# Nine small tiles instead of ten ahead of the weight tiles: where matmul operands begin in SBUF

## The chip, the core and the metric

The kernel runs on one core of a Trainium2 chip. The metric is the device time of one execution in microseconds (us); a lower time is better. A core has a matrix engine (TensorE; PE in the profile, with its weight loads as PEld), a vector engine (VectorE, DVE), an activation engine (ScalarE, ACT), GpSimd (POOL) and a queue engine that issues most transfers (SyncE, SP). They work side by side on SBUF, an on-chip memory of 128 partitions; matmul results go to PSUM. A tile takes the same byte range in every partition, and the addresses below are those within a partition.

## The reference

One layer of a streaming encoder, for 256 positions of width 2048, all in float32:

```python
x = x + 0.5 * swiglu(rms_norm(x, ffn1_norm), ffn1_w_gate, ffn1_w_up, ffn1_w_down)
h = rms_norm(x, mix_norm)
u, q, k, v = split(h @ w_in)
y_ssm = s5_mixer(u, ...)                       # diagonal complex state space, then a GLU
y_sb = stick_breaking_attention(rms_norm(q), rms_norm(k), v)
x = x + concat(rms_norm(y_ssm), rms_norm(y_sb)) @ w_out
x = x + 0.5 * swiglu(rms_norm(x, ffn2_norm), ffn2_w_gate, ffn2_w_up, ffn2_w_down)
gate = sigmoid(rms_norm(x, ple_norm) @ w_ple_gate)
x = x + rms_norm((p @ w_ple_proj) * gate, ple_post_norm)
```

The two feed-forward blocks (2048 to 5632 and back) hold most of the arithmetic, then `w_in`, `w_out` and `w_ple_gate`.

## The kernel before

Every large product is done as three products of float32r halves. A float32 value is split into a high part (rounded to float32r, a form of float32 that TensorE streams in one pass) and a low part, the rest; high x high, low x high and high x low are added up in PSUM. `split` (line 178) does it: ScalarE copies the source into the high tile (L181), VectorE subtracts that from the source into the low tile (L184). Weights come from HBM in tiles `raw` of 128 x 4 x 512 floats, one MB each, issued by SyncE; each half of such a tile becomes `whi` and `wlo` of 128 x 2 x 512. Activations stand as `nhi`/`nlo` or `hhi`/`hlo`, 128 x 4 x 256, turned so that 128 x 128 blocks of them are the stationary operand (`lhsT`) and the weights the moving one (`rhs`). In the GLU alone the weights are stationary and 256 columns of activations move (L1369, L1373, L1378).

`gemm_half` (line 298) issues, for a half weight tile, 12 matmuls of 512 columns: L305 and L306 with `whi`, L310 with `wlo`. `Seven` (from line 446) is a scheme with seven products for a 2 x 2 block of tiles, where VectorE adds up weight tiles first (L487) and the matmuls stand at L480, L481 and L483. The feed-forward blocks use both forms by turns. In each (j, t) of these loops the three lines are issued once:

```python
for j in range(2):
    for t in ts:
        nc.tensor.matmul(ps[t], lhsT=lh, rhs=hi[:, j, cols], start=start and j == 0, stop=False)
        nc.tensor.matmul(ps[t], lhsT=ll, rhs=hi[:, j, cols], start=False, stop=False)
for j in range(2):
    for t in ts:
        nc.tensor.matmul(ps[t], lhsT=lh, rhs=lo[:, j, cols], start=False, stop=stop and j == 1)
```

Smaller work on TensorE: transposes with the identity as moving operand (L392, L1207), sums over partitions with ones as moving operand (L1299), attention masks (L1234: `ident_r` stationary, `late_r` moving), and ten filler matmuls near the end (L1556: `ident_r` stationary, `pT` moving) while the last mean is worked out. GpSimd scales one 128 x 1 tile there (L1549).

**Where tiles lie.** Pools are laid out in SBUF one behind the other, in the order in which lines 52 to 56 open them, and each tile takes a multiple of 32 bytes. Ahead of the weights stand, in bytes per partition: 1024 of scratch for transfers (`dynamic_dma_scratch_size=1024`), four built-in constants of 32, then the pool `const` with `ident`, `ones`, `late_r`, `ident_r`, `tri_r`, `all_r` of 512 each, `gains` (354 floats, 1416, takes 1440) and `rho4` (128), then the pool `small`: tiles of 8 floats, 32 bytes, given out in turn by `small()` (line 82) for sums of squares, roots and the like. With ten of them the sum is 1024 + 128 + 3072 + 1440 + 128 + 320 = 6112 = 95 x 64 + 32. Every tile behind it takes a multiple of 64 bytes, and all offsets into one that a matmul uses (512 bytes for a 128-column block, 2048 for a 512-column row) are multiples of 64 as well. So in the kernel before, every weight, activation and sum that TensorE reads begins 32 bytes past a multiple of 64. The six 512-byte tiles of `const` begin at 1152 = 18 x 64 and are at multiples of 64.

Of the kernel before, what the change touches and what calls it, by code (L numbers as in the profile page):

```python
# [33 lines left out]
def layer_kernel(ctx: ExitStack, tc: tile.TileContext, a: dict, shapes: dict, out: bass.AP):  # L34
# [15 lines left out]
    assert TT == 2 and NP == 64 and HC == 16 and DH == P and NC == 64 and SW == NH * DH  # L50

    cpool = ctx.enter_context(tc.tile_pool(name="const", bufs=1))
    smp = ctx.enter_context(tc.tile_pool(name="small", bufs=10))
    wp = ctx.enter_context(tc.tile_pool(name="wts", bufs=4))
    actp = ctx.enter_context(tc.tile_pool(name="act", bufs=1))
    comp = ctx.enter_context(tc.tile_pool(name="com", bufs=1))
# [1605 lines left out]
```

## Time and profile before

| | |
|---|---|
| median of 3 runs | 1849.6 us (1848.7 to 1849.92) |
| profiled execution, its own time | 1849.88 us |
| its span, first to last instruction | 1847.8 us |
| TensorE busy | 1835.1 us, 99% of the span |
| VectorE busy | 1460.7 us, 79% |
| ScalarE busy | 1027.3 us, 56% |
| mean granted TensorE clock | 0.999 |
| HBM read | 373.46 MB, 209 GB/s over the span |

A matmul's busy time in the profile runs from its start to its modelled end and overlaps the next one's; the distance between starts is the pace. The timeline lists instructions with their start and duration in us; equal ones that follow each other are merged into one row with their number behind an x. The table of busy time by stretch gives, for a stretch of the span: its length; busy time and number of instructions (x) of PE, PEld, DVE, ACT and POOL in this order, of those engines that have any; the granted clock; the DMA engines' busy share; GB/s.

### The profile page before, as it was taken

How to read it: one execution, taken by the hardware profiler on the slowest of the kernel's cores; microseconds unless marked ns; L12 is line 12 of the kernel's file. 1: busy time of each engine (PE TensorE's matmuls, PEld its weight loads, DVE VectorE, ACT ScalarE, POOL GpSimd, SP SyncE). 2: the span in 40 equal slices, each digit the busy share in tenths (PEclk: the TensorE clock that was granted, in tenths of full speed). 3: DMA queues.
4: the chain of work that ended last, by engine and by line, in shares of the span. 5: the costliest groups of instructions: out<-in, count | busy, mean ns of one | idle time of the engine just before them, and what ended most of it. 6: DMA issues, size and time to landing. Idle time of an engine off the chain costs nothing.

```text
span 1847.8 us, 23946 instructions
## 1 busy us (share of the span) xinstructions
PE 1835.1 (99%) x9032; PEld 1518.8 (82%) x9032; DVE 1460.7 (79%) x1718; ACT 1027.3 (56%) x1187; POOL 65.1 (4%) x108
## 2 busy tenths in 40 slices
PE   9999999999999999999999999999999999999998
PEld 7888888778888888888898888888888888888887
DVE  8967664998888977687566798989898978887665
ACT  7444443655555656365685465555555555565654
POOL 0011000000000000010021000000000000000000
PEclk9999999999999999999999999999999999999999
DMA  9888868566756567675636776665656675656663
GB/s 332 283 273 281 251 213 247 178 228 203 242 189 221 193 217 249 190 263 166 216 139 218 221 266 213 242 206 198 218 198 221 208 242 187 223 190 220 207 220 125
DMA packets 232307, 406.36 MB, mean 220 GB/s; under 512 B 26784, under 2 KB 50720, under 8 KB 231904
## 3 DMA queue, kind: packets, MB, share of 16 engines
q1 hardware_dynamic: 227824, 392.81, 64.2%
q0 software_dynamic: 3648, 10.62, 1.8%
q8 instruction: 70, 1.15, 0.2%
q10 hardware_dynamic: 720, 1.41, 0.2%
q14 instruction: 45, 0.37, 0.1%
HBM read 373.46 MB, written 11.93 MB: 209 GB/s over the span
## 4 chain that ended last, share of the span: by engine, by line
PE 92%; DVE 3%; ACT 1%; DMA 1%; SPq 1%; issue 1%; DVEq 0%; ACTq 0%
PE acc L305 18%; PE acc L310 18%; PE acc L306 18%; PE aux L305 7%; PE aux L306 7%; PE aux L310 7%; PE acc L480 2%; PE acc L481 2%; PE acc L483 2%; PE aux L483 2%; PE aux L480 2%; PE aux L481 2%; SPq L1170 1%; DVE wlo L184 1%; DMA raw<-in_w_in 1%
## 5 line engine op out<-in xcount | busy, mean ns | idle before, releaser
L181 ACT CAST whi<-raw 128x1024 fp32r<-128x1024 f32 x639 | 667.5, 1051 | 679.3 <-PE acc L306 377.2
L184 DVE TENSOR_TENSOR wlo<-raw,whi 128x1024 fp32r<-128x1024 f32 x639 | 772.8, 1224 | 295.9 <-ACT whi L181 287.9
L305 PE MATMUL acc<-whi,nhi 128*128 128x512 f32 x1232 | 483.0, 392 | 2.1 <-ACT whi L181 1.6
L306 PE MATMUL acc<-whi,nlo 128*128 128x512 f32 x1232 | 480.0, 390 | 0.0
L310 PE MATMUL acc<-wlo,nhi 128*128 128x512 f32 x1232 | 340.7, 389 | 0.2 <-DVE wlo L184 0.2
L305 PEld LDWEIGHTS acc<-whi,nhi 128*128 128x128 f32 x1232 | 231.5, 188 | 52.6 <-ACT whi L181 3.1
L310 PEld LDWEIGHTS acc<-wlo,nhi 128*128 128x128 f32 x1232 | 231.3, 188 | 48.6 <-DVE wlo L184 0.6
L306 PEld LDWEIGHTS acc<-whi,nlo 128*128 128x128 f32 x1232 | 231.6, 188 | 47.0
L306 PE MATMUL acc<-whi,hlo 128*128 128x512 f32 x376 | 146.5, 390 | 0.0
L305 PE MATMUL acc<-whi,hhi 128*128 128x512 f32 x376 | 146.4, 389 | 0.0
L181 ACT CAST shi<-sum 128x1024 fp32r<-128x1024 f32 x108 | 113.5, 1052 | 43.1 <-DVE sum L487 39.4
L306 PE MATMUL aux<-whi,hlo 128*128 128x512 f32 x344 | 133.9, 389 | 0.0
L305 PE MATMUL aux<-whi,hhi 128*128 128x512 f32 x344 | 133.9, 389 | 0.0
L184 DVE TENSOR_TENSOR slo<-sum,shi 128x1024 fp32r<-128x1024 f32 x108 | 131.4, 1222 | 0.5 <-ACT shi L181 0.5
L310 PE MATMUL acc<-wlo,hhi 128*128 128x512 f32 x376 | 114.8, 390 | 0.2 <-DVE wlo L184 0.2
L310 PE MATMUL aux<-wlo,hhi 128*128 128x512 f32 x344 | 105.9, 389 | 0.0
L306 PE MATMUL aux<-whi,nlo 128*128 128x512 f32 x240 | 93.4, 389 | 0.0
L305 PE MATMUL aux<-whi,nhi 128*128 128x512 f32 x240 | 93.4, 389 | 0.0
L310 PEld LDWEIGHTS acc<-wlo,hhi 128*128 128x128 f32 x376 | 70.5, 188 | 15.5 <-DVE wlo L184 1.0
L306 PEld LDWEIGHTS acc<-whi,hlo 128*128 128x128 f32 x376 | 70.6, 188 | 14.9 <-DVE hlo L184 0.3
L305 PEld LDWEIGHTS acc<-whi,hhi 128*128 128x128 f32 x376 | 70.6, 188 | 14.6
L305 PEld LDWEIGHTS aux<-whi,hhi 128*128 128x128 f32 x344 | 64.6, 188 | 13.4
(345 smaller groups left out, 2164.8 us busy)
## 6 DMA issues: line engine op xcount, KB each, us to landing
raw<-in_ffn_w_up SPq DMA_DIRECT2D x88, 1024.0 KB, 5.9
raw<-in_ffn_w_down SPq DMA_DIRECT2D x88, 1024.0 KB, 5.1
raw<-in_ffn_w_gate SPq DMA_DIRECT2D x86, 1024.0 KB, 6.3
raw<-in_w_in SPq DMA_DIRECT2D x32, 1024.0 KB, 5.7
raw<-in_w_out SPq DMA_DIRECT2D x16, 1024.0 KB, 5.1
raw<-in_w_ple_gate SPq DMA_DIRECT2D x16, 1024.0 KB, 5.2
hT<-mid SPq DMA_DIRECT2D x160, 64.0 KB, 3.5
h<-mid SPq DMA_DIRECT2D x176, 32.0 KB, 3.7
```

The source lines that it names most:

```text
L181: copy = nc.scalar.copy(hi, src)
L184: nc.vector.tensor_tensor(out=lo, in0=src, in1=hi.bitcast(F32), op=ALU.subtract)
L305: nc.tensor.matmul(ps[t], lhsT=lh, rhs=hi[:, j, cols], start=start and j == 0, stop=False)
L306: nc.tensor.matmul(ps[t], lhsT=ll, rhs=hi[:, j, cols], start=False, stop=False)
L310: nc.tensor.matmul(ps[t], lhsT=lh, rhs=lo[:, j, cols], start=False, stop=stop and j == 1)
L480: nc.tensor.matmul(ps, lhsT=lh[j], rhs=hi[:, j], start=begin and j == 0, stop=False)
L481: nc.tensor.matmul(ps, lhsT=ll[j], rhs=hi[:, j], start=False, stop=False)
L483: nc.tensor.matmul(ps, lhsT=lh[j], rhs=lo[:, j], start=False, stop=z in final and j == 1)
L1170: nc.sync.dma_start(zt[0][p1 : p1 + HC, z], sv[p0 : p0 + HC, r % 2 * 2 + r // 2])
```

## The change

One number: the pool `small` gets nine tiles in place of ten.

```diff
     cpool = ctx.enter_context(tc.tile_pool(name="const", bufs=1))
-    smp = ctx.enter_context(tc.tile_pool(name="small", bufs=10))
+    smp = ctx.enter_context(tc.tile_pool(name="small", bufs=9))
     wp = ctx.enter_context(tc.tile_pool(name="wts", bufs=4))
```

The sum ahead of the weights becomes 6080 = 95 x 64. Every tile behind the pool moves down by 32 bytes and begins at a multiple of 64; the tiles of `const` stay where they are. The small tiles are given out in turn among nine places. The instructions, their order on every engine and their waits are those of before, but for one wait: L1549 on GpSimd, whose output tile now lies where another tile was, waits for an earlier ScalarE instruction than before.

## The prediction

> **What bounds the kernel now.** I first read the page's shares of busy time and its chain of work that ended last: whichever engine holds that chain sets the time.
>
> ```profile
> PE 1835.1 (99%) x9032; PEld 1518.8 (82%) x9032; DVE 1460.7 (79%) x1718; ACT 1027.3 (56%) x1187; POOL 65.1 (4%) x108
> ...
> PE 92%; DVE 3%; ACT 1%; DMA 1%; SPq 1%; issue 1%; DVEq 0%; ACTq 0%
> ```
>
> TensorE is it. But a pipelined matmul counts as busy past the start of the next, so busy time says nothing of pace. For pace I take a stretch without a pause from the table of busy time by stretch; its first columns are the stretch, its length, and TensorE's busy time with the number of matmuls.
>
> ```profile
> 1095.00:1515.00 420.00, 420.00 (x1853) 347.33 (x1852) 377.94 (x368) 229.93 (x237) 4.34 (x8) 1.00 0.66 217
> ```
>
> TensorE never stands still there, its granted clock is 1.00, and a matmul begins every 420.00/1853 = 0.2267 us. The timeline of TensorE shows that this is no mean of fast and slow ones. Its first column is the start:
>
> ```profile
> 1449.23 0.39 PE L483 MATMUL acc<-wlo,hhi 128*128 128x512 f32 x1
> 1449.46 0.39 PE L480 MATMUL aux<-whi,nhi 128*128 128x512 f32 x1
> 1449.69 0.39 PE L481 MATMUL aux<-whi,nlo 128*128 128x512 f32 x1
> 1449.92 0.39 PE L480 MATMUL aux<-whi,nhi 128*128 128x512 f32 x1
> 1450.14 0.39 PE L481 MATMUL aux<-whi,nlo 128*128 128x512 f32 x1
> ...
> 948.83 0.28 PE L1369 MATMUL acc<-hhi,whi 128*128 128x256 f32 x1
> ...
> 950.15 0.28 PE L1373 MATMUL acc<-hlo,whi 128*128 128x256 f32 x1
> ```
>
> Matmuls of 512 columns start every 0.227 us. The 256-column ones of the GLU (12 of them from the first row shown to the last, so 11 intervals) take 1.32/11 = 0.120 us each. From the two widths: (226.7 - 120.0)/256 = 0.4167 ns per column, and 226.7 - 512 x 0.4167 = **13.3 ns that each matmul pays whatever its width**. At this pace that is exactly 32 columns, or 128 bytes of a float32 row: two pieces of 64 bytes. All these matmuls read a moving and a stationary operand that begin 32 bytes past a multiple of 64. How much of the 13.3 ns goes with that offset is the whole question.
>
> **The change part by part.** It removes no instruction, adds none and moves none on any engine. It moves the addresses of everything allocated behind the small tiles by 32 bytes, and alters one wait.
>
> *The wait.* L1549, GpSimd's scale of a 128x1 tile in the tail, waits for an earlier ScalarE instruction than before. It waits in fact for VectorE:
>
> ```profile
> POOL sm L1549 <- DVE sq L1542: 355.0, 1, 355.0
> ```
>
> So this is worth nothing: L1542 still ends when it ends. Nine tiles in place of ten bring no other new wait.
>
> *The addresses under TensorE.* How many matmuls are concerned? The same table restricted to one line, over the whole span, first for L305, then for L480:
>
> ```profile
> 0.00:1848.00 1848.00, 863.16 (x2210) 415.13 (x2210) 1.00 0.66 220
> ...
> 0.00:1848.00 1848.00, 147.43 (x378) 70.98 (x378) 1.00 0.66 220
> ```
>
> L306 and L310 are issued as often as L305, L481 and L483 as often as L480: 3 x 2210 + 3 x 378 = 7764, of which 12 have 256 columns (the last block's second half, which `gemm_resident` does in two parts): 7752 of 512. The GLU issues L1369, L1373 and L1378 64 times each, so 192 of 256 columns.
>
> No row of before has a settled stream of 512-column float32r matmuls on operands that begin at a multiple of 64, so the saving is bounded. The **upper end** comes from the nearest streams with hardly any fixed cost, fp32 matmuls whose moving operand (the identity, the ones) begins at a multiple of 64:
>
> ```profile
> 731.31 0.93 PE L392 MATMUL aux<-ident,x 128*128 128x128 f32 x7
> ...
> 972.12 0.60 PE L1299 MATMUL aux<-ones,sqg 128*128 128x128 f32 x4
> ```
>
> The last one's own duration is in the group's row (minimum, median and maximum in ns): 0.27 us for L392, and as much for L1299.
>
> ```profile
> L392 PE MATMUL aux<-ident,x x8: 270/272/273, 731.3 to 732.1; 128*128 128x128 f32 x8
> ```
>
> So the starts lie (0.93 - 0.27)/6 = 0.110 and (0.60 - 0.27)/3 = 0.110 us apart. If such a record streams its 128 columns twice, that is 106.7 ns and 2.5 to 3 ns fixed. So at most 13.3 - 2.5 = 10.8 ns per matmul can go. These rows are another data type, though, and one of their operands does lie at the odd 32 bytes.
>
> The Trainium skill ("TensorE: Matmul & The Clock Gate", section "Back-to-back issue gap") gives N/2.4 + 2.5 ns for a warm matmul, with no term for where an operand begins; that is 215.8 ns for 512 columns where this trace has 226.7. By that figure as an estimate for the aligned kernel, the sum would be that of the upper end.
>
> The **other end** comes from the few float32r matmuls whose operands both begin at a multiple of 64 already, the masks (L1234, 256 columns read as the same 128 twice):
>
> ```profile
> 892.50 0.40 PE L1234 MATMUL aux<-late_r,ident_r 128*128 128x256 f32 x2
> 892.74 0.59 PE L1240 MATMUL aux<-q,k 128*128 128x256 f32 x2
> ```
>
> Two of them take 0.24 us, 0.120 each to within 0.005: no quicker than the misaligned GLU. They come in pairs behind other work and restart their row midway, so they don't show a settled stream, but they forbid counting on the upper end.
>
> I take a value between: **one of the two 64-byte pieces goes.** A row of 2048 bytes that begins 32 bytes off touches 33 pieces of 64 bytes, one that begins on the boundary 32; one piece is 16 columns, 6.67 ns. This reading is an inference from the fixed cost being a whole number of such pieces at both widths. It gives 7752 x 6.67 = 51.7 us and 192 x 6.67 = 1.3 us, together 53.0.
>
> *What is late next.* VectorE makes every low half of a weight tile, and is the next fullest engine:
>
> ```profile
> 340.00:510.00 170.00, 167.28 (x736) 137.88 (x736) 158.46 (x157) 94.57 (x98) 4.39 (x8) 1.00 0.68 220
> ```
>
> In 340 to 510 us VectorE is busy 158.5 of 170 (93%) and TensorE already waits 2.7; in 1095 to 1515 it is 377.9 of 420 (90%) with TensorE never idle. These 590 us hold 590/1848 of the gain, 16.9 us. With 2.9% less time VectorE would stand at 96% and 93% there. Nothing given back and all of it are the ends; I take a third, 5.6 us, since the longer stretch has no wait today.
>
> *The addresses under the others.* ScalarE, VectorE and the DMAs use the shifted tiles too. All that is not TensorE holds 8% of the chain, and DMA engines are busy 66% of the span in the rows above; a change of a few per cent either way stays under TensorE, except in the 590 us, where VectorE's spare 7 to 10% is the cover. I put nothing for them.
>
> Sum against the profiled execution (span 1847.8, its own time 1849.88; the median of the runs shown, 1849.6, is 0.3 less): 1849.9 - 53.0 + 5.6 = **1802.5**.
>
> **The rivals.**
>
> *The whole excess goes* (upper end). 10.8 x 7944 = 86 us; 590/1848 of it, 27 us, lies where VectorE is nearly full, and half of that might come back: 1849.9 - 86 + 14 = 1778, or 1764 with nothing given back. For it: the fp32 rows. Against it: the mask rows.
>
> *The change doesn't do what it says for time.* The 13.3 ns may belong to something that aligned operands pay as well, such as the load of new weights that runs beside every matmul. For it: the mask rows at 0.120. Then 1849.9 stays. The Trainium skill speaks for this one ("SBUF — State Buffer", section "Specifications (TRN2)"): it gives SBUF lines of 16 bytes, and an operand 32 bytes past a multiple of 64 begins on such a line already, so nothing would change; no row here shows the size of a line.
>
> *Slower: the stream no longer settles.* After a pause TensorE's starts are wider for some ten matmuls before they fall into 0.227:
>
> ```profile
> 153.10 0.40 PE L306 MATMUL acc<-whi,nlo 128*128 128x512 f32 x1
> ...
> 154.73 1.08 PE L310 MATMUL acc<-wlo,nhi 128*128 128x512 f32 x4
> ...
> 1838.84 2.05 PEld L1556 LDWEIGHTS aux<-pT,ident_r 128*128 128x128 f32 x9 [0.24 <-issue]
> ```
>
> From 153.10 to 154.73 there are seven intervals of 0.233. The tail's filler matmuls, whose stationary operand already begins at a multiple of 64 while the moving one doesn't, show (2.05 - 0.19)/8 = 0.2325 between weight loads, and don't settle within ten. So the pace depends on how the weight load and the moving operand meet in time, and the present 32-byte offset may be what lets them settle. If aligned streams stay at 0.233, that is 6.1 ns more: 1849.9 + 7752 x 6.1 ns = 1897. It decides as soon as the settled pace is above 0.2267. Against it: the filler's operands differ in offset from each other, the changed kernel's don't.
>
> **How the numbers follow.** One piece saved (the forecast, 1802, from 1790 to 1830 with the give-back and partial savings): 0.42. All of it (1764 to 1785): 0.25. No change, within 0.2% (3.7 us, about what a measurement of this kernel can tell from none): 0.18. Never settling, 1897: 0.15. That makes faster 0.67, same 0.18, slower 0.15. The range leaves out the last: from 1764, the upper end with nothing given back, to 1852, no change with its spread.
>
> **What would show it.** Right: in 1095 to 1515 us of the changed profile some 1909 matmuls per 420 us (0.220), GLU matmuls at 0.1133, VectorE's share up by about 3 points, small new waits of TensorE for L184 around 340 to 510. All gone: 0.216 and 0.109. No change: 0.2267 and 0.120. Slower: 0.231 or more, uneven. I am wrong in kind, not size, if the pace per matmul stays and the time moves: then another engine or the DMAs felt the addresses, and the rows of L181, L184 or the time to landing must show it.

## The result and the profile after

The changed kernel takes **1848.46 us** (median of 14 runs, 1847.95 to 1849.69), the kernel before, timed beside it, 1848.93 us (14 runs, 1848.06 to 1850.41). The ratio of the two is **0.9997, 95% interval 0.9989 to 1.0006**: no change, where 1802 was forecast. The profiled execution took 1848.89 us with a span of 1846.8.

The shares of busy time and the chain of the changed kernel stand as before: TensorE holds the chain.

```profile
PE 1833.7 (99%) x9032; PEld 1517.5 (82%) x9032; DVE 1459.7 (79%) x1718; ACT 1027.3 (56%) x1187; POOL 62.6 (3%) x108
...
PE 94%; DVE 2%; DMA 1%; SPq 1%; ACT 1%; issue 0%; DVEq 0%; ACTq 0%
```

The table by stretch answers the question directly:

```profile
340.00:510.00 170.00, 167.28 (x737) 137.79 (x737) 158.97 (x158) 94.80 (x98) 4.39 (x8) 1.00 0.67 220
1095.00:1515.00 420.00, 420.00 (x1852) 347.19 (x1851) 377.51 (x368) 230.37 (x237) 4.34 (x8) 1.00 0.66 217
```

In 1095 to 1515 us 1852 matmuls begin where 1853 began: 420.00/1852 = 0.2268 us each. In 340 to 510 there are 737 for 736. The timeline shows the single starts, of 512 columns and of the GLU's 256:

```profile
1449.11 0.39 PE L480 MATMUL aux<-whi,nhi 128*128 128x512 f32 x1
1449.33 0.39 PE L481 MATMUL aux<-whi,nlo 128*128 128x512 f32 x1
1449.56 0.39 PE L480 MATMUL aux<-whi,nhi 128*128 128x512 f32 x1
...
948.24 0.28 PE L1369 MATMUL acc<-hhi,whi 128*128 128x256 f32 x1
...
949.80 0.28 PE L1373 MATMUL acc<-hlo,whi 128*128 128x256 f32 x1
```

0.227 us again, and 1.56/13 = 0.120 for the GLU. The 13.3 ns beyond the columns are all still there; this is what the prediction gave for its rival of no change, "0.2267 and 0.120". Nothing was gained and lost again elsewhere.

For the comparisons below I sum up all distances between starts that follow a matmul of 512 columns, or of the 496 or 480 that stand for them in two runs (7773 in each trace: the 7752 large ones of the prediction, the fillers and a few more), in two parts: the mean of those up to 250 ns, which is the pace without a pause, and what the longer ones, in which TensorE waited or did other work, hold beyond that mean. Worked out from the start times in the traces, for all kernels of this study that hold the layer (the kernel before, timed again beside each of the others, took 1848.9 to 1850.0):

```
kernel         pace, ns   longer ones hold, us   time, us (median)
before           226.8          14.8             1848.93
after            226.8          14.5             1848.46
nine_odd         226.8          14.4             1849.31
unequal          232.8          12.0             1892.77
cut16            221.9          26.0             1823.72
cut32half        223.9          22.2             1834.27
quarter_half     224.0          17.6             1830.23
quarter_all      215.8          39.4             1790.4
```

### The profile page after: what moved, and what is told of

It reads as the page before. It is cut to its first block, busy times and chain, and to the rows that moved or that the text cites. A ratio compares the mean times of both kernels' runs of the same rounds, so it can differ in the third digit from the quotient of the medians.

```text
span 1846.8 us, 23946 instructions
## 1 busy us (share of the span) xinstructions
PE 1833.7 (99%) x9032; PEld 1517.5 (82%) x9032; DVE 1459.7 (79%) x1718; ACT 1027.3 (56%) x1187; POOL 62.6 (3%) x108
## 4 chain that ended last, share of the span: by engine, by line
PE 94%; DVE 2%; DMA 1%; SPq 1%; ACT 1%; issue 0%; DVEq 0%; ACTq 0%
PE acc L305 19%; PE acc L310 19%; PE acc L306 19%; PE aux L305 7%; PE aux L306 7%; PE aux L310 7%; PE acc L480 3%; PE acc L481 3%; PE acc L483 3%; PE aux L480 2%; PE aux L481 2%; PE aux L483 2%; SPq L1170 1%; DVE wlo L184 1%; DMA raw<-in_ffn_w_up 1%; PE aux L1124 0%
## 5 line engine op out<-in xcount | busy, mean ns | idle before, releaser
L184 DVE TENSOR_TENSOR wlo<-raw,whi 128x1024 fp32r<-128x1024 f32 x639 | 771.6, 1221 | 296.3 <-ACT whi L181 289.6
L305 PE MATMUL acc<-whi,nhi 128*128 128x512 f32 x1232 | 482.7, 392 | 2.6 <-ACT whi L181 1.6
L305 PEld LDWEIGHTS acc<-whi,nhi 128*128 128x128 f32 x1232 | 231.2, 188 | 53.3 <-ACT whi L181 3.2
L305 PE MATMUL acc<-whi,hhi 128*128 128x512 f32 x376 | 146.3, 389 | 0.0
L305 PE MATMUL aux<-whi,hhi 128*128 128x512 f32 x344 | 133.9, 389 | 0.0
L305 PE MATMUL aux<-whi,nhi 128*128 128x512 f32 x240 | 93.4, 389 | 0.0
L310 PEld LDWEIGHTS acc<-wlo,hhi 128*128 128x128 f32 x376 | 70.5, 188 | 15.2 <-DVE wlo L184 0.6
L306 PEld LDWEIGHTS acc<-whi,hlo 128*128 128x128 f32 x376 | 70.6, 188 | 14.8 <-DVE hlo L184 0.2
L305 PEld LDWEIGHTS acc<-whi,hhi 128*128 128x128 f32 x376 | 70.6, 188 | 14.7
L310 PEld LDWEIGHTS aux<-wlo,hhi 128*128 128x128 f32 x344 | 64.6, 188 | 13.5
```

Of the source, the lines that this page charges most:

```text
L184: nc.vector.tensor_tensor(out=lo, in0=src, in1=hi.bitcast(F32), op=ALU.subtract)
```

## Experiments

What the fixed 13.3 ns belong to had three answers left: a cost that every float32r matmul pays wherever its operands lie; a cost of lying off some boundary, hidden in the changed kernel by something else that the change did; or a cost that hangs on how the two operands lie **to each other**. The last was open because the change moves both by the same 32 bytes. By the order and sizes of the pools `whi`, `wlo`, `nhi`, `nlo`, `hhi`, `hlo`, `shi` and `slo` all begin at 224 modulo 256 before (`whi` at 47072, `nhi` at 79840) and at 192 after; the tiles of `const` begin at 128 in both.

Six of the runs are streams by themselves: a loop of matmuls on a moving operand `mv` and a stationary one `st`, each in one tile, with no layer around them, each run once. Blocks of one kind follow each other, so a block's pace is the distance from its row's start to the next row's, over its count. The code of these streams is shown shortened: letters stand for the offsets of each loop, and `...` for what stays as it was.

**m_offsets.** Both operands begin at 128 modulo 256; `a` and `b` shift them, in floats.

```diff
+for i in range(200):
+    mm(ps, lhsT=st[:, i%4*128 + a : i%4*128 + a + 128], rhs=mv[:, i%4*512 + b : i%4*512 + b + 512], start=True, stop=True)
```

> No layer is computed: eight streams of 200 float32r matmuls of 512 columns, alike but for where the moving and the stationary operand begin past a multiple of 64 bytes (moving/stationary: 0/0, 32/32, 32/0, 0/32, 4/0, 0/4, 16/16, 60/60 bytes). Theory A, the 13.3 ns belong to something every float32r matmul pays (its weight load, say): all eight settle at 0.2267 us. Theory B, only offsets within a 16-byte line matter: the three with 4 or 60 bytes are slower by one line, 4 columns, 1.7 ns, the other five stand at 0.2267. Theory C, the filler's 0.2325 was its unequal offsets: 32/0 and 0/32 stand at 0.2325, the equal ones at 0.2267.

The timeline of its TensorE; the blocks are, in bytes of moving/stationary shift, 0/0, 32/32, 32/0, 0/32, 4/0, 0/4, 16/16, 60/60:

```profile
9.74 48.17 PE L35 MATMUL b<-mv,st 128*128 128x512 f32 x200 [9.74 <-ACT st L28]
57.75 45.53 PE L37 MATMUL b<-mv,st 128*128 128x512 f32 x200
103.11 46.82 PE L39 MATMUL b<-mv,st 128*128 128x512 f32 x200
149.77 46.83 PE L41 MATMUL b<-mv,st 128*128 128x512 f32 x200
196.44 47.50 PE L43 MATMUL b<-mv,st 128*128 128x512 f32 x200
243.78 46.65 PE L45 MATMUL b<-mv,st 128*128 128x512 f32 x200
```

32/32 takes (103.11 - 57.75)/200 = 0.2268 us, and the first block, once settled, 0.2267: shifting both by 32 bytes does nothing. Shifting one alone costs: 32/0 0.2333, 0/32 0.2333, 4/0 0.2367, 0/4 0.2324. So theory A (all alike) falls, and B with it, since 32/0 is slow; C, that unequal beginnings cost, holds on the 32-byte grid. Off it, 16/16 and 60/60 take 0.2333 though they are equal; m_grid comes back to them. At 32 bytes the relation counts, not the boundary.

**m_shapes.** No shifts; the number of stationary columns, of moving columns, the PSUM bank, accumulation and the data type vary instead.

```diff
+mm(ps[:64], lhsT=st[:, i%4*128 : i%4*128 + 64], rhs=...)      # L41; L43 with 32
+mm(ps[:, :384], ..., rhs=mv[:, i%4*512 : i%4*512 + 384])      # L45; L47 with 128
+mm(banks[i % 8], ...)                                         # L49; L51 accumulates, L53 keeps one st
+mm(ps, lhsT=stb[...], rhs=mvb[...])                           # L55 bfloat16; L57 with 256 columns, L59 with 64 stationary
```

> No layer is computed: streams of 200 matmuls, all operands at multiples of 64 bytes. If the fixed 13.3 ns come from the 128-column weight load, they shrink with the columns loaded: 0.2267 us with 128, about 0.220 with 64, 0.2167 with 32 (512 moving columns). If they belong to the moving float32r stream, all three stand at 0.2267 and only bf16 is quicker. If they belong to writing one PSUM bank over and over, going round eight banks takes them away (0.216), and accumulating keeps or raises them. 384 columns: 0.1733 if the cost is fixed; 128 columns: 0.0667 if fixed, more if the weight load itself then sets the pace. Loading the same weights again and again: 0.2267. bf16, 512 and 256 columns: 0.216 and 0.109 if the fixed cost is float32r's alone.

```profile
58.20 46.17 PE L41 MATMUL b<-mv,st 128*64 128x512 f32 x200
104.21 46.51 PE L43 MATMUL b<-mv,st 128*32 128x512 f32 x200
150.56 34.84 PE L45 MATMUL b<-mv,st 128*128 128x384 f32 x200
185.23 22.44 PE L47 MATMUL b<-mv,st 128*128 128x128 f32 x200
207.51 45.58 PE L49 MATMUL b<-mv,st 128*128 128x512 f32 x200
252.93 45.50 PE L51 MATMUL b<-mv,st 128*128 128x512 f32 x200
298.26 45.49 PE L53 MATMUL b<-mv,st 128*128 128x512 f32 x200
343.60 43.34 PE L55 MATMUL b<-mvb,stb 128*128 128x512 bf16 x200
386.77 22.00 PE L57 MATMUL b<-mvb,stb 128*128 128x256 bf16 x200
408.70 43.35 PE L59 MATMUL b<-mvb,stb 128*64 128x512 bf16 x200
```

Eight banks (0.2271), accumulation (0.2267) and one stationary block for all (0.2267; it is still loaded anew before every matmul) change nothing. 384 columns take (185.23 - 150.56)/200 = 0.1733, once more 13.3 ns beyond their columns; 128 take 0.1114, far above the 0.0667 that a fixed 13.3 would give, so the 13.3 ns do not hold at every width. In bfloat16 the same 512 columns take (386.77 - 343.60)/200 = 0.2159 and 256 take 0.1097: 2.5 to 3 ns beyond the columns. So, of the 13.3 ns, 10.8 go with float32r. The Trainium skill ("TensorE: Matmul & The Clock Gate", section "Back-to-back issue gap") gives N/2.4 + 2.5 ns as the gap of an isolated warm matmul; its 215.8 for 512 columns agrees with the bfloat16 stream and not with the 226.7 of float32r. Fewer stationary columns don't help: 64 take 0.2300, 32 take 0.2318.

**m_streams.** What the moving operand reads varies.

```diff
+rhs=mv[:, c : c + 128].unsqueeze(1).to_broadcast([P, 4, 128])   # L39: the same 128 columns, four times over
+rhs=mv[:, c : c + 128].unsqueeze(2).to_broadcast([P, 128, 4])   # L41: each of 128 columns four times running
+rhs=mv[:, c : c + 1].to_broadcast([P, 512])                     # L43: one column
+rhs=mv[:, d : d + 1024].rearrange('p (n k) -> p n k', k=2)[:, :, 0]   # L45: every second column
+lhsT=st[:, c : c + 1].to_broadcast([P, 128])                    # L47: one stationary column
+rhs=mv[:, c : c + 504]                                          # L49; L51 496, L53 480, L55 448 columns; L57 plain float32
```

> No layer is computed: streams of 200 float32r matmuls, operands at multiples of 64 bytes: plain; the moving operand the same 128 columns four times; each of 128 columns four times running; one column 512 times; every second column; the stationary operand one column 128 times; 504, 496, 480 and 448 moving columns; and plain float32. If the 13.3 ns are two read streams meeting in memory, reading fewer moving or stationary bytes takes them away or changes them (0.216 to 0.2267), and reading every second column raises them. If they are a fixed start of a float32r matmul, all 512-column streams stand at 0.2267. By cut16, 496 columns don't settle: 0.223 to 0.225 in place of 0.220; 480 and 448, multiples of 32, settle at 0.2133 and 0.2000. float32, two records of two passes: 0.4267 plus some 2.5 ns a record.

```profile
20.85 45.50 PE L37 MATMUL b<-mv,st 128*128 128x512 f32 x200
66.18 45.49 PE L39 MATMUL b<-mv,st 128*128 128x512 f32 x200
111.52 43.33 PE L41 MATMUL b<-mv,st 128*128 128x512 f32 x200
154.68 43.33 PE L43 MATMUL b<-mv,st 128*128 128x512 f32 x200
197.85 90.83 PE L45 MATMUL b<-mv,st 128*128 128x512 f32 x200
288.50 46.41 PE L47 MATMUL b<-mv,st 128*128 128x512 f32 x200
334.75 45.51 PE L49 MATMUL b<-mv,st 128*128 128x504 f32 x200
380.10 44.83 PE L51 MATMUL b<-mv,st 128*128 128x496 f32 x200
424.76 43.49 PE L53 MATMUL b<-mv,st 128*128 128x480 f32 x200
468.10 40.70 PE L55 MATMUL b<-mv,st 128*128 128x448 f32 x200
508.63 171.83 PE L57 MATMUL b<-src 128*128 128x512 f32 x400
```

Where a column is used four times running, the 10.8 ns are gone: (154.68 - 111.52)/200 = 0.2158, the bfloat16 pace. Where the same 128 columns come four times over, so that each step reads another column, they stay: 0.2267. The weight load is the same in both, so the excess goes with new moving bytes in every column. Plain float32 (L57, two records a matmul) takes 171.83/400 = 0.43, settled 0.4292 a record: 2.5 ns beyond twice 213.3. If a record reads its columns once at half the pace, that fits: the excess needs four new bytes per column at full speed. If it streams them twice, as the prediction assumed of L392, float32 asks for as many bytes as float32r and doesn't pay, and then new bytes alone are not the reason. No run here tells the two apart. Every second column halves the pace (0.4533); a stationary operand that is one column 128 times gives 0.2312, no gain.

The lengths missed what was expected: 504 columns take as long as 512 (0.2267), 496 take 0.2233, 480 0.2167 and 448 0.2027. The first three carry 16.7 ns beyond their columns and the last 16.0, where 256, 384 and 512 carry 13.3.

**m_grid** and **m_grid32.** Every pair of eight shifts, 80 matmuls each: first shifts of 0, 4, 8, 16, 32, 48, 64 and 96 bytes, then of 0 to 224 in steps of 32. The edit is that of m_offsets with these `a` and `b`.

> No layer is computed: 64 streams of 80 float32r matmuls of 512 columns; the moving and the stationary operand each begin 0, 4, 8, 16, 32, 48, 64 or 96 bytes past a multiple of 128. Theory D, only the difference of the two beginnings modulo 64 counts, if both are multiples of 32: (0,0), (32,32), (0,64), (64,0), (32,96) and their like settle at 0.2267 us, all others lie between 0.232 and 0.237. Rival, what counts is that both begin at the same byte: (0,64) and (32,96) are slow too, (16,16) was slow by its starting phase and is quick in places. Is there a pair below 0.2267? Theory A (a fixed cost) says none, theory D leaves it open.

> No layer is computed: 64 streams of 80 float32r matmuls of 512 columns; the moving and the stationary operand each begin 0, 32, 64 up to 224 bytes past a multiple of 128, the beginnings that tiles can have. Theory D as the first grid left it: equal beginnings modulo 128 settle at 0.2267 us, (0,0) as (128,0) or (160,32); unequal ones lie at 0.2289 to 0.2367. Rival: 128 and 0 differ as 64 and 0 did, and only the same byte or the same 256 is quick. None below 0.2267 by either.

Three rows of m_grid32: moving/stationary 0/0, 0/32 and 64/64. Each merges 80 matmuls; the difference shows in the second column, the time from first start to last end.

```profile
21.69 18.30 PE L36 MATMUL b<-mv,st 128*128 128x512 f32 x80
39.83 18.82 PE L37 MATMUL b<-mv,st 128*128 128x512 f32 x80
...
355.72 18.30 PE L54 MATMUL b<-mv,st 128*128 128x512 f32 x80
```

The settled pace of all 64 in ns (mean of the last 40 distances of a block); rows are the shift of the moving operand, columns that of the stationary one:

```
m_grid32    0     32     64     96    128    160    192    224
  0       226.7  233.3  233.3  234.3  233.3  233.3  228.8  233.3
 32       233.3  226.7  233.3  233.3  234.3  233.3  233.3  228.8
 64       228.8  233.3  226.7  233.3  233.3  234.3  233.3  233.3
 96       233.3  228.8  233.3  226.7  233.3  233.3  234.2  233.3
128       233.3  233.3  228.8  233.3  226.7  233.3  233.3  234.3
160       234.3  232.5  233.4  228.8  233.3  226.7  233.3  233.3
192       233.3  234.2  233.3  233.3  228.8  233.3  226.7  233.3
224       233.3  233.3  234.3  233.3  233.3  228.8  233.3  226.7
```

Within 1 ns the table goes round: a cell hangs on the difference of the two shifts modulo 256. (The theory that 128 bytes are the period falls: 0/128 takes 233.3.) Equal beginnings give 226.7, a moving operand 64 bytes ahead 228.8, all else 232.5 to 234.3. Equality counts only in steps of 32 bytes: in m_grid 4/4 gives 239.2, 8/8 232.9, 16/16 230.0, 48/48 231.1, and unequal pairs there lie anywhere from 226.7 (such as 16/4 and 64/48) to 240.0. Off that grid the addresses don't settle the matter alone: 16/16 took 233.3 in m_offsets and 230.0 here. **No pair of either table is below 226.7.** Both kernels of this case have all matmuls of their large products on the diagonal, one step apart on it.

**unequal.** The changed kernel with one unused tile of 32 bytes between weights and activations: the weights stay at 192 modulo 256, all behind them goes to 224.

```diff
+    ctx.enter_context(tc.tile_pool(name="gap", bufs=1)).tile([P, 8], F32, name="gap")
     actp = ctx.enter_context(tc.tile_pool(name="act", bufs=1))
```

> The changed kernel with a tile of 32 bytes nobody uses behind the weights: 7050 of its large matmuls then move weights that begin at a multiple of 64 past stationary activations that begin 32 bytes off. If unequal beginnings cost what the streams showed (0.2333 against 0.2267), it takes 7050 x 6.67 ns = 47 us more, 1896. If the streams' result doesn't carry over to the kernel, it stays at 1849.

1892.77 us (1892.71 to 1892.9) against 1849.48 of before: ratio 1.0235, interval 1.022 to 1.025, **43.3 us slower**.

```profile
1095.00:1515.00 420.00, 420.00 (x1809) 339.80 (x1808) 376.79 (x365) 229.29 (x236) 2.28 (x5) 1.00 0.65 210
```

TensorE is busy all the time and starts only 1809: 420/1809 = 0.2322 us. By the table of distances 7773 x (232.8 - 226.8) ns = 46.8 us, less 2.5 in the longer ones. m_grid32 has 233.3 for this pair (0/32). The same trace holds its own control: `shi` and `slo` lie behind the gap like the activations, so their matmuls keep equal beginnings. Of the distances up to 250 ns, the 7054 behind matmuls that move `whi` or `wlo` have a mean of 233.3, the 642 behind those that move `shi` or `slo` 227.9. So 32 bytes do cost 6 ns a matmul in this kernel, if they move one operand and not the other.

**nine_odd.** Nine small tiles, and 32 unused bytes ahead of the weights: everything lies as before, only the tenth small tile is missing.

```diff
+    ctx.enter_context(tc.tile_pool(name="gap", bufs=1)).tile([P, 8], F32, name="gap")
     wp = ctx.enter_context(tc.tile_pool(name="wts", bufs=4))
```

> Nine small tiles, and 32 bytes nobody uses behind them: every weight, activation and sum begins 32 bytes past a multiple of 64 again, as in the kernel before, so only the number of small tiles is changed. If neither part of the change does anything: the time of the kernel before, within 0.2%. If nine tiles cost what the even beginnings win: some us above it.

1849.31 us (1848.57 to 1851.34) against 1849.21: ratio 1.0001, interval 0.9992 to 1.001. Nine tiles in place of ten cost nothing that this shows (the interval allows 2 us), so the result isn't a gain by the addresses that the scarcer tiles took back.

**m_cols.** If the excess were the weight load's own reads, it should fall with the number of stationary columns. The moving operand stays at 0; the stationary one has 96, 64 or 32 columns at the shifts of m_grid32.

> No layer is computed: float32r matmuls of 512 moving columns with 96, 64 or 32 stationary columns, the stationary operand beginning 0, 32, up to 224 bytes further than the moving one (modulo 256). If the 10.8 ns above a bf16 matmul are the weight load's own reads, the best of the eight beginnings falls with the columns loaded: 0.2240 us with 96, 0.2213 with 64, 0.2185 with 32. If the weight load only has to fall in step and costs a fixed delay, the best stays at 0.2267 for all three.

```
m_cols      0     32     64     96    128    160    192    224
96 cols   230.0  228.9  228.3  230.7  226.7  231.2  233.3  233.3
64 cols   230.0  231.7  231.2  231.4  229.3  231.2  228.3  230.8
32 cols   231.7  240.0  231.7  230.6  230.7  233.3  231.7  233.3
```

The best cell is 226.7 and no lower than with 128; fewer columns only settle worse. That idea falls. The rule of equal beginnings doesn't carry over either: with 96 columns they give 230.0, and 226.7 comes with the stationary operand 128 bytes ahead.

**cut16.** The kernel before, with the last 16 of 512 columns left out of the large matmuls except the one that begins a sum: a saving of 6.67 ns each, the size that the forecast had.

```diff
+CUT = 16
...
+        short = slice(0, NB - CUT) if cols == slice(0, NB) else cols
+        n = short.stop - short.start
...
-                nc.tensor.matmul(ps[t], lhsT=ll, rhs=hi[:, j, cols], start=False, stop=False)
+                nc.tensor.matmul(ps[t][:, :n], lhsT=ll, rhs=hi[:, j, short], start=False, stop=False)
```

> The kernel before with 16 columns fewer in 7529 of its 7752 large 512-column matmuls (all but those that open a PSUM bank; the last 16 columns of every block miss part of their sum): just the 6.67 ns a matmul that the prediction counted on, 50.2 us of TensorE's time in all. If pace per matmul sets the time, it falls to between 1799 (nothing given back) and 1815 (all given back in the two stretches where VectorE is nearly full); the prediction's third gives 1804. If something else were the bound, it would stay near 1849.

1823.72 us (1822.51 to 1826.04) against 1849.41: ratio 0.9863, interval 0.9846 to 0.9879, 25.7 us of the 50.2. Two losses: the pace falls to 221.9 ns only (of 7529 distances behind a 496-column matmul 3612 are 220 ns, nearly all of the rest longer; a stream of 496 columns alone has 223.3), worth 7773 x 4.9 = 38 us; and the longer distances take back 26.0 - 14.8 = 11 us. The second shows where VectorE is nearly full:

```profile
1095.00:1515.00 420.00, 414.69 (x1859) 348.13 (x1858) 380.01 (x372) 231.87 (x238) 4.34 (x8) 1.00 0.66 216
```

TensorE, never idle there before, now waits 5.3 us.

**cut32half.** The same with 480 columns in the matmuls of `j == 1` and 512 in those of `j == 0`.

> The kernel before with 32 columns fewer in every large matmul of the second of two 128-row blocks (half of them, 3876; the last 32 columns of every block miss part of their sum). If 480 columns settle as 512 do, each takes 13.3 ns less, 51.7 us in all, the saving that the prediction counted on. All through to the end: 1798; a third of the share in the two stretches with VectorE nearly full given back: 1803; all of that share: 1814. If two lengths by turns don't settle, the pace stays above and the time with it.

1834.27 us (1832.24 to 1835.52) against 1849.48: ratio 0.9917, interval 0.99 to 0.9933, 15.2 us of 51.7. The pace is 223.9 ns where the expectation had (226.7 + 213.3)/2 = 220. Half of what is missing is the length itself: 480 columns alone take 216.7 (m_streams), so 221.7 were due. The other 2.2 ns come with the turns: in this trace the 480-column matmuls have 217.6 and the 512-column ones 230.1.

**quarter_all** and **quarter_half.** The changed kernel, with each large matmul's 512 moving columns replaced by its first 128, each four times running, in all or only in those of `j == 1`: the full upper end without touching a wait.

```diff
+    def four(u, j, cols=slice(0, NB)):
...
+        return w[:, : NB // 4].unsqueeze(2).to_broadcast([P, NB // 4, 4])
...
-                nc.tensor.matmul(ps[t], lhsT=lh, rhs=hi[:, j, cols], start=start and j == 0, stop=False)
+                nc.tensor.matmul(ps[t], lhsT=lh, rhs=four(hi, j, cols), start=start and j == 0, stop=False)
```

> The changed kernel with every large matmul moving 128 columns of its weights, each four times running, in place of 512 different ones (so the products are of the wrong columns); instructions, their order, the tiles and the transfers stay. The streams showed 0.2158 us for such a matmul against 0.2267, so TensorE's own time falls by 7752 x 10.8 ns = 84 us, the upper end that the prediction weighed. If pace per matmul sets the time and all of it gets through: 1848.5 - 84 = 1765. With half of the share in the two stretches where VectorE is nearly full given back, as the prediction's rival had it: 1778. With all of that share given back: 1791.

> The same for the second of two 128-row blocks alone, half of the large matmuls: 3876 x 10.8 ns = 42 us, near the saving that was forecast. All through: 1807; a third of the two stretches' share given back: 1811; all of it: 1820. If plain matmuls by turns with quick ones don't settle at 0.2267, up to 6.6 ns of each plain one is lost again: as late as 1832.

quarter_all takes 1790.4 us (1788.88 to 1791.22) against 1849.98: ratio 0.9675, interval 0.9659 to 0.9691, 59.6 us. The matmuls do what they should, 7773 x (226.8 - 215.8) = 85 us, and 39.4 - 14.5 = **25 us come back** as pauses. Set against the changed kernel matmul by matmul, half of it, 12.6 us, comes at the matmuls of the two stretches that the prediction named, and the other half outside them. The same two stretches, then the chief waits of TensorE (in total, times, longest, us):

```profile
340.00:510.00 170.00, 165.20 (x757) 141.65 (x756) 161.02 (x160) 98.81 (x102) 4.39 (x8) 1.00 0.69 223
1095.00:1515.00 420.00, 412.48 (x1900) 357.97 (x1899) 380.38 (x372) 233.39 (x241) 4.33 (x8) 1.00 0.69 223
```

```profile
PE aux L489 <- DVE slo L184: 7.6, 13, 1.2
PE acc L311 <- ACT whi L181: 4.7, 4, 1.5
PE aux L486 <- ACT shi L181: 4.0, 3, 1.5
```

Instead of 420/0.2158 = 1946 matmuls 1900 begin in the longer stretch, and TensorE now waits for VectorE's low halves and ScalarE's high ones (L311, L486 and L489 are L305, L480 and L483 of before).

quarter_half takes 1830.23 us (1829.79 to 1830.82) against 1849.98: ratio 0.9892, interval 0.9878 to 0.9907, some 20 us of 42. Here little comes back in pauses (17.6 against 14.5), but the plain matmuls lose their step. Rows from its timeline; L486 and L487 come in fours, two plain (`j == 0`) and then two quick ones:

```profile
1201.68 0.39 PE L486 MATMUL acc<-shi,nhi 128*128 128x512 f32 x1
1201.91 0.40 PE L487 MATMUL acc<-shi,nlo 128*128 128x512 f32 x1
1202.14 0.38 PE L486 MATMUL acc<-shi,nhi 128*128 128x512 f32 x1
1202.36 0.38 PE L487 MATMUL acc<-shi,nlo 128*128 128x512 f32 x1
```

From start to start the plain ones take 0.23 and 0.23, the first quick one 0.22; over the whole trace 215 or 216 ns for the quick and mostly 231 to 235 for the plain, where a stream of plain ones alone has 226.7. The mean of all is 224.0 where (226.8 + 215.8)/2 = 221.3 were due.

## Why the prediction was wrong

**The bound** was named rightly: the time follows TensorE's pace in all eight kernels of the table, and where pauses take part of it back (at most 25 us, quarter_all) TensorE waits for VectorE and ScalarE, as the prediction had warned of VectorE.

**The wait** was priced rightly at nothing. In the changed kernel L1549 waits as before for VectorE (355.0 us then):

```profile
POOL sm L1549 <- DVE sq L1542: 354.4, 1, 354.4
```

**The addresses under the other engines**, put at nothing, cost nothing: VectorE's low half of a weight tile takes a mean of 1221 ns (1224 before) and the total of its busy time is within 1.0 us of before; ScalarE's total is 1027.3 us in both, and a tile of `in_ffn_w_up` lands after 5.8 us (5.9 before).

```profile
L184 DVE TENSOR_TENSOR wlo<-raw,whi 128x1024 fp32r<-128x1024 f32 x639 | 771.6, 1221 | 296.3 <-ACT whi L181 289.6 <-DMA dd<-in_ssm_d_laid 2.5 <-PE aux L863 1.7
```

**The step that failed** is "I take a value between: one of the two 64-byte pieces goes". From 13.3 ns being 32 columns' time it concluded that the cost came in two pieces of 64 bytes and that one of them was due to the offset; that made the term of 53.0 us. None is, and the term measures nothing: 0.2267 us before, 0.2268 after. m_offsets has 0.2267 at 0/0 and at 32/32 alike, and the four pairs on m_grid32's diagonal that begin 32 past a multiple of 64 show the same 226.7 as the four on one. That a number is a whole multiple of something was no evidence for a mechanism, since 2.5 of the 13.3 ns are paid in bfloat16 too and 10.8 are not a multiple of 6.67.

**The upper end** leaned on fp32 rows, with 2.5 to 3 ns fixed. They were right for fp32 (m_streams, L57: 2.5) and said nothing of float32r, whose other 10.8 ns go with new bytes in every column (m_streams, L39 against L41).

**The other end was the answer.** The mask rows, the only float32r matmuls of before with both operands on multiples of 64, said 0.120 from rows rounded to 0.01 us, and that is what aligned GLU matmuls take. The agreement is in part luck: by the exact start times the eight of them take 117 to 119 ns, between the GLU's 120 and the 113.3 that one piece would have given, and pairs behind other work don't settle, as the prediction said. Still they were the nearest rows by data type, width and address, and they lie nearer to no change than to the value taken.

**The rival of no change** came true. Its reason, that something which aligned operands pay as well lies behind the 13.3 ns, is what the runs show; the load of new weights by itself is not that something, since fewer weight columns (m_cols) leave the excess and the same load beside a repeated moving column (m_streams, L41) doesn't have it. The Trainium skill's 16-byte lines ("SBUF — State Buffer", section "Specifications (TRN2)") led to the right time by luck, for they don't give the paces here: 0/32 has both operands on such lines and costs 6.6 ns.

**The rival of a slower stream** did not come true, but it looked in the right place: the pace does hang on how the two operands lie, and its own "against" named the condition, beginnings that differ from each other, which the change doesn't make. unequal makes them, and pays 43 us. Its witness, the filler at L1556, is even predicted by m_grid32. Its moving operand `pT` lies 96 bytes ahead of `ident_r` before (224 against 128 modulo 256) and 64 after. The table says 233.3 and 228.8; the trace of before had 0.2325, the one of after has (2.02 - 0.19)/8 = 0.2288:

```profile
1837.87 2.02 PEld L1556 LDWEIGHTS aux<-pT,ident_r 128*128 128x128 f32 x9 [0.24 <-issue]
```

These ten matmuls are among the few of 512 columns whose operands the change moved against each other, and the pace followed. In unequal, where `pT` is 96 bytes ahead again, they have 0.2324.

**What is late next** was not put to the test by the change. quarter_all tests it on the whole excess: there the prediction let half of the two stretches' share come back, 14 of 27 us, and 12.6 did. What it left out is the rest of the kernel, where it put nothing and another 12 us came back. Had the 86 us been there, the time would have been some 1790, not 1778. cut16, with 38 us saved in the pace, gives back 11 us, 7.6 of them in the two stretches, so a third there (5.6 us of a saving of 53) was too little as well.

**What stays open.** Why equal beginnings modulo 256 settle at 226.7 and not at 215.8. That the weight load's reads and the moving operand's meet is argued from the pace's dependence on the stationary address (226.7 to 234.3); but the excess doesn't shrink with the stationary columns, so it isn't simply those reads taking turns. Some of it may be a fixed cost of the 4-byte stream. No run separates the two, and no run found 512 different float32r columns below 226.7.

## What to carry to other kernels

Before aligning operands to a boundary, work out where the two operands of a matmul begin relative to each other: in float32r, 512 moving and 128 stationary columns keep their best pace when both begin at the same byte modulo 256 on a 32-byte grid, and a stray 32-byte tile between the pools costs 6 ns a matmul, 2.3% here. A saving per matmul need not arrive whole: lengths just under 512 carry some 3 ns more than 512 does, two kinds of matmul by turns lose 2 to 3 ns more, so that about half of it vanished in the pace of cut32half and quarter_half, and pauses for the other engines take a further part. And where a row of the same kind exists, however short, its value comes before an inference from a round number.

## What the runs showed that I had not expected

Equal beginnings are best for 512 columns, not for every width. In unequal the GLU's 256-column matmuls, activations 32 bytes ahead of the weights, are quicker than in the kernels before and after, (971.16 - 969.76)/12 = 0.1167 against 0.120:

```profile
969.76 0.28 PE L1374 MATMUL acc<-hlo,whi 128*128 128x256 f32 x1
...
971.16 0.28 PE L1374 MATMUL acc<-hlo,whi 128*128 128x256 f32 x1
```

The 192 of them are worth only 0.6 us; 256 columns were not tried on a grid.

The first dozen matmuls of a stream kernel, behind some 10 us without any, are far slower. In m_offsets a first distance of 591 ns is followed by 11 of 426 to 427, then one of 288, then eight between 224 and 236, and only then 226.7. The slow stretch and the settled one in the table by stretch:

```profile
9.50:15.00 5.50, 5.26 (x12) 4.18 (x13) 3.33 (x6) 0.19 (x1) 0.00 (x0) 1.00 0.25 106
15.50:57.00 41.50, 41.50 (x184) 34.33 (x184) 0.00 (x0) 0.00 (x0) 0.00 (x0) 1.00 0.02 7
```

The granted clock stands at 1.00 in both, so it doesn't show this. 426.7 ns is twice the 213.3 ns of 512 columns. If that is half speed, which the clock column doesn't confirm, there is no excess at half speed, and it goes with full speed as well as with new bytes per column.
